# A two-layer hybrid trunk: the last 64 of 320 small triangular inverses go from VectorE to GpSimd

## The chip, the cores and the metric

The kernel runs on one core of a Trainium2 chip. A core has a matrix engine (TensorE, PE in the rows below), a vector engine (VectorE, DVE), an activation engine (ScalarE, ACT), a general-purpose vector engine (GpSimd, POOL), and SyncE (SP), which here issues the DMA transfers. Each engine works through its own list of instructions in order and waits on semaphores for the others. The metric is device time in microseconds (us), the median of several runs; lower is better.

## The reference, cut to what matters

Two layers are applied to 1024 latent tokens and 256 context tokens of width 1024. Each layer has a token mixer with three parallel head groups, an output projection, and a SwiGLU block. Of the mixer two groups matter here: the windowed attention, whose queries and keys are rotated, and a recurrence with a 64x64 state per head, in both directions.

```
def apply_rope(x, cos, sin):
    ...
    out = jnp.stack([x1 * c - x2 * s, x2 * c + x1 * s], axis=-2)
...
    def update(S, w_t, k_t, v_t, kk_t, a_t):
        sa = jnp.einsum('bhvk,bhk->bhv', S, kk_t)
        return (S * w_t[:, :, None, :] - sa[..., None] * (kk_t * a_t)[:, :, None, :]
                + v_t[..., None] * k_t[:, :, None, :])
...
    _, y_f = wkv_scan(wX[:, :, 0], kdX[:, :, 0], vX, kkX, aX[:, :, 0], Sc_f, False, rX)
    _, y_b = wkv_scan(wX[:, :, 1], kdX[:, :, 1], vX, kkX, aX[:, :, 1], Sc_b, True, rX)
```

The kernel doesn't step token by token. It takes 64 tokens at a time; inside such a chunk the updates are coupled by a unit lower triangular matrix, and its inverse turns the chunk into a few matmuls. The inverses are built from the inverses of 32x32 diagonal blocks, 320 of them per layer.

## The kernel before, in words

In each layer the mixer runs in this order: projections; attention over 16 to 20 units (one tile of 128 query tokens and one key head each); the recurrence over 80 units; the output projection. The recurrence has four chains (two head pairs by two directions), each of five groups of 256 tokens, each group of four chunks: unit 0 to 19 is chain 0, 60 to 79 chain 3. So one unit is one chunk for a pair of heads, and group 5 holds units 20 to 23, group 6 units 24 to 27, group 7 units 28 to 31.

A unit has four stages that are issued at different steps: u0 (the matmuls that start a unit, their masks on DVE at L1230 and L1233), u1, u4 and u5 (the state update, whose scaling on DVE is L1267). Tiles of a group are `bC`: three sets of them are used in turn. `beta_load` issues a group's loads on SP (L1201 and L1203 from `cb`, L1204 from `tb`, L1210 from `vt`), and it may be issued only when the inverses of its chain are joined; `own` then copies parts of them on POOL (L1182). `chunk_set` makes the constant parts of a set (DVE L1165, POOL L1167 and L1174).

Two lanes of background work are woven into attention and recurrence. The second lane makes the inverses: `elim(b0, n)` loads `n` blocks, one block per partition (`eL<-Ld`, L662), lays an identity into `eX` (POOL L663, L664), and runs 31 steps of forward elimination. Step j multiplies a column of the block by a row of the inverse so far (L671, of (31-j)(j+1) elements per partition) and subtracts the product (L673). Each of the 62 operations needs the result of the one before it. Then `eX` is stored (L675), its transpose copied to `eL` (L676), and that is stored (L677). `join_load` reads the results back (L696 to L699), and `join` puts pairs of 32x32 blocks together on PE (tile `gg` during the recurrence, 32x32 matmuls) and stores them to `tb` (L718). `inverses` calls elim for blocks 0 to 127, 128 to 255, and, ahead of join 6, for blocks 256 to 319. Joins 6 and 7, which read these, belong to chain 3 alone.

Attention of unit n takes its queries from `rot`: two multiplications on DVE (L959, L960) and one addition on POOL (L962, 128x256). PE transposes the rotated queries (L1053), then makes the scores, DVE their maximum (L1085), ACT the exponential, DVE part of the scaling (L1109); PE transposes the result (L1132) and multiplies by the values.

What the program text writes is not the order in which the engines work. A scheduler sets the order of each engine's list when the kernel is built, from its own idea of what an instruction costs and needs; on the chip each list is then run as it stands.

Of the kernel before, what the change touches and what calls it, by code (L numbers as in the profile page):

```python
# [13 lines left out]
ALU = mybir.AluOpType  # L14
# [80 lines left out]
def trunk(ctx: ExitStack, tc: tile.TileContext, x, ctxt, cc, w_mod, pp, w_in, w_out, lng, lnb, sgw, sink,  # L95
          w2, a2, g2, w_gu, w_down, cst, rope, out, dbg=None):
    nc = tc.nc
    V, S, G, T, D = nc.vector, nc.scalar, nc.gpsimd, nc.tensor, nc.sync
# [14 lines left out]
    def alloc(name, dt=F32):  # L113
        i = free.popleft()
        return Slot(sp.tile([128, NTOK], dt, tag=f"s{i}", name=nm(name)), i)

    def rel(*ss):
        for s in ss:
            free.append(s.i)
# [420 lines left out]
    def layer(l):  # L540
# [114 lines left out]
            rel(L1, L2, O1, O2)  # L655
            yield AC

        def elim(b0, n):

            ML = alloc("eL")  # L660
            MX = alloc("eX")
            D.dma_start(ML.t[:n, :1024], Ld[b0:b0 + n].rearrange("s i j -> s (i j)"))  # L662
            G.memset(MX.t[:n, :1024], 0.0)  # L663
            G.memset(MX.t[:n, 0:1024:33], 1.0)  # L664
            Lm = ML.t[:n, :1024].rearrange("p (i j) -> p i j", j=32)
            X = MX.t[:n, :1024].rearrange("p (i j) -> p i j", j=32)
            yield EW
            for j in range(31):
                r, c = 31 - j, j + 1
                tmp = ML.t[:n, 1024:1024 + r * c].rearrange("p (i j) -> p i j", j=c)  # L670
                V.tensor_tensor(tmp, Lm[:, j + 1:, j:j + 1].to_broadcast([n, r, c]),  # L671
                                X[:, j:j + 1, :c].to_broadcast([n, r, c]), op=ALU.mult)
                V.tensor_tensor(X[:, j + 1:, :c], X[:, j + 1:, :c], tmp, op=ALU.subtract)  # L673
                yield EC
            D.dma_start(Xd[0, b0:b0 + n, :], MX.t[:n, :1024])  # L675
            V.tensor_copy(Lm, X.rearrange("p i j -> p j i"))  # L676
            D.dma_start(Xd[1, b0:b0 + n, :], ML.t[:n, :1024])  # L677
            rel(ML, MX)
            yield
# [3 lines left out]
        def join_load(n):  # L683

            ci, c0 = n // 2, 10 * (n % 2)
            J = alloc("jT")

            def v(b, c, w=320):
                return J.t[h32[b], c:c + w].rearrange("p (c j) -> p c j", c=10)

            def xb(z, b):
                m = (ci * 20 + c0) * 4
                return Xd[z, m:m + 40].rearrange("(c b) (i j) -> b i c j", b=4, i=32)[b]
            for lo, hi in ((0, 1), (2, 3)):
                G.memset(v(lo, 0, 640)[:, :, 32:64], 0.0)
                D.dma_start(v(hi, 640), c10(Ad[ci][h32[hi], c0 * 32:c0 * 32 + 320]))  # L696
                D.dma_start(v(hi, 960), xb(1, hi))
                D.dma_start(v(lo, 0, 640)[:, :, 0:32], xb(0, lo))
                D.dma_start(v(hi, 0, 640)[:, :, 32:64], xb(0, hi))  # L699
            return n, J, v  # L700

        def join(n, J, v):
            for st_ in range(2):
                ps = x_t()
                for c in range(10):
                    for lo, hi in ((0, 1), (2, 3)):
                        o = slice(32 * c, 32 * c + 32)
                        if st_ == 0:
                            mm(ps[h32[lo], o], v(hi, 640)[:, c, :], v(hi, 960)[:, c, :])
                        else:  # L710
                            mm(ps[h32[hi], o], v(lo, 640)[:, c, :], v(lo, 0, 640)[:, c, 0:32])
                yield
                for lo, hi in ((0, 1), (2, 3)):
                    if st_ == 0:
                        S.activation(v(lo, 640), c10(ps[h32[lo], 0:320]), AF.Copy)
                    else:
                        S.activation(v(hi, 0, 640)[:, :, 0:32], c10(ps[h32[hi], 0:320]), AF.Copy, scale=-1.0)
            D.dma_start(tb[n // 2][:, (n % 2) * 640:(n % 2) * 640 + 640], J.t[:, 0:640])  # L718
            rel(J)
# [9 lines left out]
        def inverses():  # L729
            for pair in range(2):  # L730
                while ("alpha", pair) not in rw:
                    yield
                yield from elim(128 * pair, 128)
            j = join_load(0)
            for n in range(8):
                if n == HB:
                    while "beta" not in rw:
                        yield
                    j = join_load(n)
                if n == 6:  # L740
                    yield from elim(256, 64)
                    j = join_load(n)
                i, j = j, join_load(n + 1) if n not in (HB - 1, 5, 7) else None
                yield JW
                yield from join(*i)
                if n % 2:
                    rw["join", n // 2] = True
# [64 lines left out]
        def mix_done(i, raw, dst, begun=False):  # L812
            lat = i < 3 and not full
            token_mix(l, i, raw.t, dst.t, lat, begun)
            rel(raw)
            if i in (3, 4):
                bgq.appendleft(kk_norm(i - 3, dst))
            elif i in (0, 1):
                spill(dst, i, 2, 256 if lat else 0)
                rw["r", i] = True  # L820
            elif i == 7:
                S.activation(dst.t, dst.t, AF.Tanh)
                rw["wd"] = dst
            elif i == 8:
                rw["ad"] = dst
            elif i in (5, 6):
                D.dma_start(rd[i - 5], dst.t)
                bgq.appendleft(v_turn(i - 5, dst))
            else:
                c0 = 256 if lat else 0  # L830
                D.dma_start(rd[2][:, c0:], dst.t[:, c0:])
                rel(dst)
            if i == 0:
                bgq.append(alphas())
                elq.append(inverses())
# [547 lines left out]
        for n in range(len(ul) + max(s[1] for s in LG)):  # L1383
# [4 lines left out]
            for s, lag in LG:  # L1388
                m = n - lag
                if 0 <= m < len(ul):  # L1390
                    ci, gi, c = ul[m]
# [409 lines left out]
        tmp, aux = ft, alloc("aux")  # L1801
# [176 lines left out]
```

## Time and profile before

| what | value |
| --- | --- |
| time, median of 3 runs | 3263.41 us (3260.81 to 3267.21) |
| the profiled execution's own time | 3260.54 us |
| its span, first to last instruction | 3258.5 us |
| mean granted TensorE clock | 0.987 of full speed |
| busy share PE / DVE / ACT / POOL | 97% / 62% / 43% / 16% |
| elim of the last 64 blocks, layer 0 | 530.3 to about 587 us |
| elim of the last 64 blocks, layer 1 | 2259.4 to about 2308 us |
| last unit's query rotation on POOL, layer 0 | 541.20 us |
| first unit of the recurrence on PE, layer 0 / 1 | 566.35 / 2259.16 us |

Busy shares are averages over the whole span. In the rows below, times are us from the start of the span; a form such as 64x207 is 64 partitions by 207 elements, and a row's bracket gives how long the engine had been idle and what ended that.

### The profile page before, as it was taken

What the parts mean: (1) busy time and instruction counts of PE and PEld (TensorE: products, weight loads), DVE (VectorE), ACT (ScalarE), POOL (GpSimd) and SP (SyncE); (2) the same over time, 40 slices, a digit from 0 to 9 for tenths busy, and PEclk for the clock granted to TensorE, in tenths of its full rate; (3) what the DMA queues carried; (4) which work ended last, traced back from release to release, by engine and by line L of the source; (5) the groups of instructions that cost most, each with busy time, mean ns of one, the idle gap of its engine ahead of it and who ended that gap; (6) DMA issues with size and microseconds to landing.
All of it is one profiled execution on the core that took longest, in us unless ns stands there. A gap on an engine that the chain in (4) does not pass through costs nothing.

```text
span 3258.5 us, 51944 instructions
## 1 busy us (share of the span) xinstructions
PE 3152.4 (97%) x19892; PEld 2560.8 (79%) x19892; DVE 2004.0 (62%) x3966; ACT 1389.1 (43%) x2874; POOL 527.9 (16%) x598
## 2 busy tenths in 40 slices
PE   7999999999999999999999999999899999999998
PEld 4868887777788888886687788887677788888887
DVE  3448878775465555554455656886665666666556
ACT  4455577664332222222112556576564423333211
POOL 2300101232012222210001220111122122231000
PEclk9999999999999999999999999998999999999999
DMA  6477223346512122235722357313445222223332
GB/s 223 147 237 246 72 78 95 105 132 207 199 49 68 64 72 70 70 132 198 250 86 91 112 176 235 124 54 91 119 134 195 72 78 82 87 80 134 99 102 97
DMA packets 395175, 403.95 MB, mean 124 GB/s; under 512 B 113456, under 2 KB 334640, under 8 KB 394928
## 3 DMA queue, kind: packets, MB, share of 16 engines
q1 hardware_dynamic: 394928, 400.64, 38.3%
q8 instruction: 157, 2.57, 0.3%
q14 instruction: 90, 0.74, 0.1%
HBM read 279.97 MB, written 120.59 MB: 123 GB/s over the span
## 4 chain that ended last, share of the span: by engine, by line
PE 66%; DVE 6%; ACT 2%; DMA 1%; issue 1%; POOL 1%; SPq 0%; DVEq 0%; POOLq 0%; ACTq 0%
PE dd L148 25%; PE mm L148 19%; PE xx L148 15%; PE u L148 4%; PE mm L1132 1%; PE gg L148 0%; DVE yac L1711 0%; DVE eX L673 0%; POOL ss L180 0%; DVE eL L671 0%; DVE xr L1740 0%; DVE mx L483 0%; DMA ar<-actd 0%; PE xx L1132 0%; DVE yac L1739 0%
## 5 line engine op out<-in xcount | busy, mean ns | idle before, releaser
L148 PE MATMUL mm<-h,wh 128*128 128x512 f32 (+1 forms) x1424 | 421.7, 379 | 3.3 <-ACT ntmp L402 2.3
L148 PE MATMUL mm<-wh,h 128*128 128x256 f32 x1472 | 324.7, 295 | 1.3 <-ACT gel L872 0.6
L148 PE MATMUL dd<-h,wh 128*128 128x256 f32 (+1 forms) x1312 | 323.1, 337 | 2.7 <-DVE h L411 2.0
L148 PEld LDWEIGHTS mm<-h,wh 128*128 128x128 f32 x1424 | 258.5, 190 | 63.0 <-issue 13.7
L148 PE MATMUL mm<-h,wl 128*128 128x512 f32 (+1 forms) x712 | 266.3, 374 | 1.1 <-DVE wl L233 1.1
L148 PEld LDWEIGHTS mm<-wh,h 128*128 128x128 f32 x1472 | 247.8, 192 | 18.7 <-issue 14.7
L148 PEld LDWEIGHTS dd<-h,wh 128*128 128x128 f32 x1312 | 228.7, 191 | 31.2 <-DVE h L411 2.5
L1589 ACT ACTIVATE wh<-wq 128x1024 fp32r<-128x1024 f32 x114 | 121.0, 1062 | 302.8 <-PE dd L148 113.9
L148 PE MATMUL dd<-h,wl 128*128 128x256 f32 (+1 forms) x656 | 220.1, 336 | 0.0
L1590 DVE TENSOR_TENSOR wl<-wq,wh 128x1024 fp32r<-128x1024 f32 x114 | 141.2, 1238 | 114.8 <-ACT wh L1589 114.8
L148 PE MATMUL mm<-wl,h 128*128 128x256 f32 x736 | 210.3, 286 | 0.5 <-DVE wl L233 0.5
L148 PE MATMUL dd<-tt,wh 128*128 128x512 f32 x608 | 188.1, 391 | 0.0
L180 POOL TENSOR_TENSOR ss<-ss,mh_sb 128x1 f32<-128x1 f32 x74 | 50.4, 682 | 842.4 <-DVE ss L379 840.1
L148 PEld LDWEIGHTS mm<-h,wl 128*128 128x128 f32 x712 | 135.1, 190 | 25.2 <-DVE wl L233 1.4
L1711 DVE TENSOR_TENSOR yac<-yac,mm 128x512 f32<-128x512 f32 x126 | 86.4, 686 | 107.9 <-PE mm L148 107.5
L148 PEld LDWEIGHTS mm<-wl,h 128*128 128x128 f32 x736 | 142.0, 193 | 2.5 <-issue 1.4
L1711 DVE TENSOR_TENSOR yac<-yac,xx 128x512 f32<-128x512 f32 x126 | 86.3, 685 | 91.2 <-PE xx L148 91.1
L1579 POOL TENSOR_TENSOR wq<-wu 128x512 f32<-128x512 f32 x38 | 49.2, 1295 | 562.1 <-DVE wl L1590 478.1
L148 PEld LDWEIGHTS dd<-h,wl 128*128 128x128 f32 x656 | 125.3, 191 | 12.5
L148 PE MATMUL u<-bC,bC 128*128 128x128 f32 (+1 forms) x640 | 124.2, 313 | 9.5 <-DVE bC L1233 6.3
L148 PEld LDWEIGHTS dd<-tt,wh 128*128 128x128 f32 x608 | 111.7, 188 | 21.3
L148 PE MATMUL dd<-tt,wl 128*128 128x512 f32 x304 | 118.3, 389 | 0.0
(372 smaller groups left out, 7779.7 us busy)
## 6 DMA issues: line engine op xcount, KB each, us to landing
wm<-in_w_mod SPq DMA_DIRECT2D x80, 512.0 KB, 5.4
wr<-in_w_down SPq DMA_DIRECT2D x44, 512.0 KB, 4.4
wr<-in_w_in SPq DMA_DIRECT2D x38, 512.0 KB, 4.4
cb<-ao SPq DMA_DIRECT2D x76, 256.0 KB, 3.0
wu<-in_w_gu SPq DMA_DIRECT2D x38, 512.0 KB, 3.7
wq<-in_w_gu SPq DMA_DIRECT2D x38, 512.0 KB, 3.7
ao<-rk SPq DMA_DIRECT2D x58, 256.0 KB, 3.8
xs<-xr SPq DMA_DIRECT2D x28, 512.0 KB, 2.6
```

Source lines behind the costliest of these rows:

```text
L148: T.matmul(o, lhsT=lhsT, rhs=rhs, start=start, stop=stop, skip_group_check=parts)
L180: G.tensor_tensor(dst, src, mh[:, :n], op=ALU.pow)
L1132: T.transpose(ps[:, z * 128:(z + 1) * 128], P[i // 2].t[:, c:c + 128], ident)
L1579: G.tensor_tensor(a[:, 0:512], u[:, 0:512], u[:, 512:1024], op=ALU.add)
L1589: S.activation(w.hi[i], raw[i], AF.Copy)
L1590: V.tensor_tensor(w.lo[i], raw[i], f32(w.hi[i]), op=ALU.subtract)
L1711: V.tensor_tensor(yac[t].t[:, c], yac[t].t[:, c], ps, op=ALU.add)
```

## The change

`elim` gets the engine as an argument, and the call for the last 64 blocks passes GpSimd, in both layers. The two other calls are unchanged.

```
-        def elim(b0, n):
+        def elim(b0, n, E=V):
...
-                V.tensor_tensor(tmp, Lm[:, j + 1:, j:j + 1].to_broadcast([n, r, c]),
+                E.tensor_tensor(tmp, Lm[:, j + 1:, j:j + 1].to_broadcast([n, r, c]),
                                 X[:, j:j + 1, :c].to_broadcast([n, r, c]), op=ALU.mult)
-                V.tensor_tensor(X[:, j + 1:, :c], X[:, j + 1:, :c], tmp, op=ALU.subtract)
+                E.tensor_tensor(X[:, j + 1:, :c], X[:, j + 1:, :c], tmp, op=ALU.subtract)
...
-            V.tensor_copy(Lm, X.rearrange("p i j -> p j i"))
+            E.tensor_copy(Lm, X.rearrange("p i j -> p j i"))
...
                 if n == 6:
-                    yield from elim(256, 64)
+                    yield from elim(256, 64, G)
```

The scheduler sets new orders on every engine. Three places matter for what follows. The first is POOL's list in layer 0, at the end of attention, as the difference between the two lists. The list enters this piece with 36 of the 62 operations of elim already behind the memsets of `eX`; `q` is the query tile of the last attention unit.

```order
+L671 TENSOR_TENSOR eL_5868<-eL_5868,eX_5869 64x247
+L673 TENSOR_TENSOR eX_5869<-eX_5869,eL_5868 64x13x19
 L962 TENSOR_TENSOR q_3391<-q_3391 128x256
 L1182 COPY bC_6059<-bC_6062 64x2x4x64
 L1182 COPY bC_6060<-bC_6062 64x2x4x64
+L671 TENSOR_TENSOR eL_5868<-eL_5868,eX_5869 64x240
+L673 TENSOR_TENSOR eX_5869<-eX_5869,eL_5868 64x12x20
 L1182 COPY bC_6011<-bC_6014 64x2x4x64
```

So 38 operations of elim now stand ahead of the last unit's rotation, and 24 behind it, where there were none before.

The second is PE's list of the changed kernel at the same place: `xx_6044` takes the transposed queries of that last unit, `dd` are scores and `P` the probabilities of the unit before it.

```order
L148 MATMUL xx_5923<-PT_5959,Vt_2904 64x256 x4
L148 MATMUL xx_5923<-PT_5985,Vt_2904 64x256 x2
L1053 MATMUL xx_6044<-cst_sb,q_3391 128x128 x4
L148 MATMUL dd_6024<-kh_4595,qs_3392 128x384
L148 MATMUL dd_6024<-kh_4595,qs_3392 128x256
L148 MATMUL dd_6024<-kl_4596,qs_3392 128x384
L148 MATMUL dd_6024<-kl_4596,qs_3392 128x256
L1132 MATMUL mm_6052<-cst_sb,P_5876 128x128
```

The transposes stand where they stood before, ahead of the remaining scores of the unit before and of everything that follows.

The third is SP's list in layer 1, some 20 units into the recurrence, as a difference. `bC_21582` and `bC_21583` are tiles of group 5, `Xd` is where elim stores its results.

```order
+L1201 DMA bC_21582<-cb_16396 64x8x64
+L675 DMA Xd_16402<-eX_21657 64x1024
+L677 DMA Xd_16402<-eL_21656 64x1024
+L1201 DMA bC_21582<-cb_16396 64x8x64
+L1203 DMA bC_21583<-cb_16396 128x256
 L1204 DMA bC_3130_22012<-tb_16400 128x256
 L1210 DMA bC_3130_22012<-vt_16395 64x4x128
-L1201 DMA bC_21582<-cb_16396 64x8x64 x2
-L1203 DMA bC_21583<-cb_16396 128x256
```

Half of group 5's loads now stand behind the stores of elim's results. Further on, group 6's loads stood ahead of those stores and now stand behind the store of join 6 (L718), and group 7's moved behind the store of join 7. On PE, in the same stretch, the 80 small matmuls of joins 6 and 7 now all stand ahead of unit 24's first matmul:

```order
+L148 MATMUL gg_22091<-jT_22044 32x32 x19
+L148 MATMUL u_3197_22442<-bC_3130_22012,U_21591 64x64 x2
+L148 MATMUL gg_22114<-jT_22044 32x32 x20
+L148 MATMUL u_3201_22463<-bC_3130_22012,U_21591 64x64 x2
+L148 MATMUL gg_22190<-jT_22055 32x32 x20
+L148 MATMUL gg_22213<-jT_22055 32x32 x20
+L148 MATMUL u_3189_22401<-bC_21221,bC_21220 128x128 x2
```

The last row is the first of unit 24; before, the joins' matmuls lay between the stages of units 24 to 27.

## Rows read from the trace of the kernel before

**Rows 1.** The page, part 1: busy time, share of the span, instructions of each engine
```profile
PE 3152.4 (97%) x19892; PEld 2560.8 (79%) x19892; DVE 2004.0 (62%) x3966; ACT 1389.1 (43%) x2874; POOL 527.9 (16%) x598
```

**Rows 2.** Windows: length, busy PE PEld DVE ACT POOL, clock, DMA share, GB/s
```profile
2279.90:2309.10 29.20, 23.13 (x205) 17.67 (x206) 27.67 (x98) 14.05 (x52) 4.61 (x7) 0.97 0.50 137
588.00:601.00 13.00, 13.00 (x123) 9.75 (x121) 8.26 (x32) 7.72 (x31) 0.20 (x1) 1.00 0.31 54
```

**Rows 3.** Timeline of DVE, L1267, layer 0, units 0, 6, 12, 22: start, duration
```profile
573.29 0.28 DVE L1267 TENSOR_SCALAR bC<-u,pc 64x64 f32<-64x64 f32 x1
...
588.49 0.28 DVE L1267 TENSOR_SCALAR bC<-u,pc 64x64 f32<-64x64 f32 x1 [0.33 <-PE u L148]
...
600.96 0.28 DVE L1267 TENSOR_SCALAR bC<-u,pc 64x64 f32<-64x64 f32 x1
...
628.51 0.28 DVE L1267 TENSOR_SCALAR bC<-u,pc 64x64 f32<-64x64 f32 x1 [0.65 <-PE u L148]
```

**Rows 4.** Windows, DVE's work on eX alone: length, busy, clock, DMA share, GB/s
```profile
530.20:587.00 56.80, 21.79 (x63) 1.00 0.48 137
2259.30:2308.30 49.00, 21.64 (x63) 0.79 0.44 124
```

**Rows 5.** Timeline of POOL, layer 0, end of attention
```profile
529.86 0.38 POOL L664 MEMSET eX<- 64x32 f32 x1
531.32 0.24 POOL L1167 COPY bC<-cst_sb 128x64 f32<-128x64 f32 x1 [1.08 <-PE mm L148]
...
536.33 1.41 POOL L1174 COPY bC<-cst_sb 64x512 f32<-64x512 f32 x1 [2.87 <-PE mm L148]
...
541.20 0.73 POOL L962 TENSOR_TENSOR q<-q 128x256 f32<-128x256 f32 x1 [3.16 <-DVE q L960]
...
559.16 0.61 POOL L1174 COPY bC<-cst_sb 64x512 f32<-64x512 f32 x1 [5.05 <-ACT P L1098]
```

**Rows 6.** Timeline of POOL: two-input instructions, back to back
```profile
113.24 0.74 POOL L891 TENSOR_TENSOR v<-v,gw 128x256 f32<-128x256 f32 x1 [0.38 <-ACT v L890]
114.06 0.74 POOL L892 TENSOR_TENSOR v<-v,gw 128x256 f32<-128x256 f32 x1
...
969.73 1.29 POOL L1579 TENSOR_TENSOR wq<-wu 128x512 f32<-128x512 f32 x1 [42.35 <-DVE tt L1550]
971.10 1.30 POOL L1580 TENSOR_TENSOR wq<-wq,wq 128x512 f32<-128x512 f32 x1
```

**Rows 7.** POOL's groups by line: busy us, mean ns, idle before
```profile
L1182 POOL COPY bC<-bC 64x512 f32<-64x512 f32 x72 | 46.7, 649 | 129.8 <-PE u L148 70.3 <-DMA bC<-cb 56.2 <-issue 0.9
L1182 POOL COPY bC<-bC 64x256 f32<-64x256 f32 x8 | 3.4, 424 | 6.1 <-PE u L148 5.9
```

**Rows 8.** Timeline of PE, layer 0: last queries transposed, first unit
```profile
542.88 0.49 PE L1053 MATMUL xx<-cst_sb,q 128*128 128x128 f32 x3
...
566.35 1.16 PE L148 MATMUL u<-bC,bC 128*128 128x128 f32 x8
```

**Rows 9.** Timeline of DVE, layer 1: L1267, ten units apart
```profile
2279.89 0.28 DVE L1267 TENSOR_SCALAR bC<-u,pc 64x64 f32<-64x64 f32 x1 [1.39 <-PE u L148]
...
2309.08 0.28 DVE L1267 TENSOR_SCALAR bC<-u,pc 64x64 f32<-64x64 f32 x1
```

**Rows 10.** Timeline of SP's queue, layer 1
```profile
2307.09 0.49 SPq L675 DMA_DIRECT2D Xd<-eX  x1
...
2328.86 0.34 SPq L718 DMA_DIRECT2D tb<-jT  x1
```

**Rows 11.** Timeline of DVE, layer 1: first mask of units 24 and 28
```profile
2324.21 0.29 DVE L1230 TENSOR_TENSOR U<-u,cst_sb 128x128 f32<-128x128 f32 x1 [0.35 <-PE u L148]
...
2342.28 0.29 DVE L1230 TENSOR_TENSOR U<-u,cst_sb 128x128 f32<-128x128 f32 x1 [3.60 <-PE u L148]
```

**Rows 12.** Windows, layer 1, around unit 28: columns as in Rows 2
```profile
2335.00:2340.00 5.00, 2.42 (x66) 1.86 (x60) 1.12 (x4) 3.33 (x12) 0.00 (x0) 0.95 0.36 116
2340.00:2345.00 5.00, 3.98 (x18) 3.43 (x19) 1.78 (x7) 0.54 (x2) 2.44 (x4) 0.50 0.81 215
```

## The prediction, made before the changed kernel had run

> **What bounds the kernel now.** I read the page's busy shares first, then the windows around the two stretches in which the last 64 blocks are eliminated, then the timelines of the engines there. PE is busy 97% of the span and POOL 16% [rows 1], but that is an average: the change touches about 57 us in layer 0 and 49 us in layer 1 [rows 4], and what it is worth is read there. In layer 1 the elimination runs beside the first 20 units of the recurrence. DVE is busy 27.67 of 29.20 us, PE 23.13 [rows 2]: DVE is the bound, and ten units take 2309.08 - 2279.89 = 29.2 us, 2.92 each [rows 9]. Where no elimination is left, in layer 0 from unit 6 on, PE is busy 13.00 of 13 us [rows 2] and six units take 600.96 - 588.49 = 12.5 us, 2.08 each; the six before, with the end of the elimination in them, took 15.2 us, 2.53 each [rows 3]. In layer 0 most of the elimination lies ahead of the recurrence, beside the last attention units.
>
> **Part 1, what DVE is rid of.** 63 instructions, 21.8 us in layer 0 and 21.6 us in layer 1 [rows 4]. In layer 0 units 0 to 22 took 628.51 - 573.29 = 55.2 us [rows 3]; 22 units at the PE-bound pace would take 45.8, a gain of up to 9.4. The joins that stretched the later ones stay, so I take 7. In layer 1 the ten units at 2.92 would save 10 x 0.84 = 8.4 us at that pace, as far as the units may run ahead (part 4).
>
> **Part 2, what POOL is given.** No row shows these operations on POOL, so I bound them by the nearest. The operations of step j have (31-j)(j+1) elements: 62 of them with 10,912 elements together, of which the first 38 have 7,220. Two-input instructions follow each other on POOL by 0.82 us at 256 elements and 1.37 at 512 [rows 6], so one costs 0.28 + 0.00213 n us. That makes 62 x 0.28 + 10,912 x 0.00213 = 40.6 us per layer, against DVE's 21.7, and 26.0 us for the first 38. The lower bound is the one-input copy, 424 ns at 256 and 649 at 512 [rows 7], 0.20 + 0.00088 n, about 12.7 us for the first 38 and some 20 for all. These operations have inner rows of 1 to 31 elements, half of them broadcast, where the nearest rows have long ones; for that, and for DVE beside it, I take one and a half times the middle as the upper bound, 61 us and 39. I take 40.6: the operation has two inputs, as the rows of 6 have.
>
> **Part 3, who waits in layer 0.** 38 of the 62 now stand ahead of the last unit's rotation. POOL is free for them at 529.86 + 0.38 = 530.24 [rows 5]. With 26.0 us of them, two copies of 0.24 and one of 0.61 between [rows 5] and 0.73 for the rotation itself, it ends at 558.1, where it ended at 541.9. Beside DVE a copy of this kind took 1.41 us instead of 0.61 [rows 5]; I add one such delay, 0.8, and some slack, and take 560. Queued behind the rotation are two copies of `own`; behind its reader, the transposes on PE, stands everything that is left of attention: remaining scores of the unit before, probabilities, values. PE is in order and can do none of it. The transposes began at 542.88 [rows 8], so they come 17.1 us late. From them to the recurrence's first matmul there were 23.5 us [rows 8]; DVE is rid of 8 us of elimination in these, and a part of what the softmax waits for, I take 21. So the first unit starts at 581 instead of 566.35, 14.6 us late. The idle PE costs clock: in layer 1, after 5 us with PE busy 2.42, the granted clock was 0.50 for 5 us in which PE was busy 3.98 [rows 12], which cost about 2 us of work; after 17 idle us I take 3. Layer 0: 14.6 + 3 - 7 = +10.6.
>
> The Trainium skill's page "SBUF — State Buffer", section "Who interferes with whom", holds that a DVE instruction with two SBUF inputs contends with a GpSimd instruction that reads SBUF, and that in a two-port mode whoever issues first holds the ports for the whole instruction. The 1.41 us copy ran beside a DVE subtraction with two SBUF inputs, so the row agrees. By the page alone each of DVE's scalings and subtractions in this stretch could be added to POOL's chain, an estimate of some 4 us in place of the 0.8; the sum would then be +13 instead of +10. I go by the row.
>
> **Part 4, who waits in layer 1.** The elimination starts at about 2259.4 there, behind the load of its blocks. With 40.6 us of it and four 0.65 us copies of `own` between [rows 7] it ends at 2302.6, and the first store leaves at 2302.8, where it left at 2307.09 [rows 10]. So the results are ready 4 us sooner, though POOL needs twice as long as DVE, because the interleaving no longer spreads them. But the units are quicker too: at 2.08 from unit 8 on, unit 20 wants its loads at about 2310, and half of group 5's now wait behind the two stores. The transposing copy (1.1 us at the rate of [rows 7]) ends at 2304, and with the same 5 us the loads land at about 2309: just in time. Group 6's loads wait for join 6's store, which needs loads of `jT` and two rounds of 32x32 matmuls with ACT copies between. Before, that store left 2328.86 - 2307.09 = 21.8 us after the first store of elim [rows 10]; from 2302.8 that gives 2324.6, and with some 5 us, which I take for the loads behind it, unit 24's first mask comes at about 2330, where it was at 2324.21; unit 28, which stalled 3.60 us for loads behind join 7's store, at 2342.28 [rows 11], comes at about 2341. What DVE's relief wins ahead of unit 20 is waited for at unit 24, and the stall at unit 28 shrinks: I take -1 for layer 1.
>
> **Sum.** +10.6 - 1 = +9.6 us on the profiled execution's 3260.54, 3270. The median of the runs is 2.9 us above the profiled execution, so I predict 3273 us.
>
> **Rivals.**
>
> POOL is as quick on these as on copies. Then the 38 operations take 12.7 us, the rotation ends at 530.2 + 12.7 + 1.1 + 0.7 = 544.7, 3 us late, and the shorter chain behind it makes up for that; layer 0 wins the 7 us, and layer 1, whose results are ready at about 2282, before any load waits for them, some 4. That is -11, 3252 us, faster. It decides from a mean of about 0.42 us per operation ahead of the rotation (548 less 1.8 less 530.2, over 38): up to 548 the delay is no longer than the 7 us won. For it speaks that one-input rows are this short [rows 7], against it that all two-input rows of POOL are slower [rows 6]. The Trainium skill's page "GPSIMD Engine Reference", section "Elementwise — side-by-side cycle accounting", puts a two-input operation at about 2.6 cycles per element, a floor set by its read port; rows 6 agree with that in slope, 2.13 ns per element, and so it speaks against this rival, an estimate of 23.6 us for the elements alone.
>
> POOL is slower than its long rows suggest, by half: 39 us ahead of the rotation, which ends at 572, 30 us late; the first unit comes 27 us late, with the clock +30, less 7 is +23. In layer 1 the elimination ends at 2323, joins 6 and 7 hold unit 24 until about 2350, and some 6 of these 25 us come back at unit 28: +19. Together +42, 3304 us. For it speak the short broadcast rows, for which the trace has no example; against it, that DVE takes the same short rows without a penalty that shows.
>
> The recurrence gives everything back. The late start stands, but the chain behind the transposes shrinks to 19 (DVE and POOL no longer share the elimination there), all units run at 2.08 (-9.4), and layer 1 wins 4: 17.1 - 4.5 + 3 - 9.4 - 4 = +2, about 3264. For it speaks that PE is the bound as soon as the elimination is gone [rows 2]; against it, that the joins still have to be fitted in.
>
> **How the numbers follow.** The forecast has 0.55, with its own range 3262 to 3284; the quick POOL 0.12, the slow POOL 0.13, the recurrence that gives all back 0.20. A measurement of this kernel can tell about 0.2%, 6.5 us, from no change. Faster comes from the quick POOL and the edge of the last rival, 0.14; no change from most of the last rival and the lower third of the forecast, 0.32; slower 0.54. The range 3252 to 3298 reaches down to the quick POOL and most of the way to the slow one.
>
> **What would show it.** The rotation L962 of layer 0's last unit near 559, not 541; PE idle ahead of L1053 by some 13 to 17 us, and a row of granted clock 0.5 behind it; the first unit near 581 to 584; units at about 2.1 us from the start. On POOL, L671 and L673 following each other by 0.28 + 0.00213 n, 0.82 at 256 elements. In layer 1 `Xd<-eX` issued near 2303, unit 24's first mask near 2330, relative to a first unit at 2259. The forecast is wrong if POOL's spacing is under 0.45 or over 0.95 on average ahead of the rotation, if the scheduler's order let PE work on other tiles while it waits for the rotation, or if unit 24 is not held by the joins.

## The result, and the profile after

The changed kernel takes 3279.12 us (median of 6 runs, 3272.47 to 3292.63) against 3263.09 us before (3255.66 to 3267.21): ratio 1.0055, 95% interval 1.0039 to 1.0070: slower by 16 us in the medians, by some 18 in the ratio. The forecast was slower, 3273 us, +9.6 on the profiled execution.

The profiled execution of the changed kernel is the longest of its six, 3292.6 us, span 3290.5. Of the 32 us between the two spans 9.0 lie ahead of everything the change touches (the rotation ahead of the elimination starts at 536.86 instead of 527.84) and 7.0 between the recurrences, so I compare the lengths of stages, not absolute times. Busy shares say little, as before; the page's part 1:

```profile
PE 3166.1 (96%) x19892; PEld 2574.4 (78%) x19892; DVE 1969.4 (60%) x3840; ACT 1386.9 (42%) x2874; POOL 590.7 (18%) x724
```

The timeline of POOL at the end of layer 0's attention answers to [rows 5] and, for the spacing, to [rows 6]:

```profile
539.34 0.25 POOL L671 TENSOR_TENSOR eL<-eL,eX 64x31 f32<-64x31 f32 x1
...
545.69 1.40 POOL L673 TENSOR_TENSOR eX<-eX,eL 64x175 f32<-64x175 f32 x1
...
559.51 0.64 POOL L671 TENSOR_TENSOR eL<-eL,eX 64x256 f32<-64x256 f32 x1
560.22 0.72 POOL L673 TENSOR_TENSOR eX<-eX,eL 64x256 f32<-64x256 f32 x1
561.02 0.63 POOL L671 TENSOR_TENSOR eL<-eL,eX 64x255 f32<-64x255 f32 x1
...
565.24 0.71 POOL L962 TENSOR_TENSOR q<-q 128x256 f32<-128x256 f32 x1
```

The rotation ends 26.6 us after the elimination has begun; at 256 elements two operations take 1.51 us. Then the timeline of PE, the answer to [rows 8]:

```profile
566.01 1.12 PE L1053 MATMUL xx<-cst_sb,q 128*128 128x128 f32 x4 [13.27 <-POOL q L962]
...
595.23 3.68 PE L148 MATMUL xx<-PT,Vt 128*64 128x256 f32 x16 [7.13 <-ACT PT L1137]
598.84 1.18 PE L148 MATMUL u<-bC,bC 128*128 128x128 f32 x8
```

These are two waits, and only the first was forecast. The second is followed back through the timelines of ACT, POOL and SP:

```profile
594.09 0.60 ACT L1313 ACTIVATE gsx<-gsx,hw 128x256 f32<-128x256 f32 x1 [7.42 <-POOL gsx L1308]
594.60 1.06 ACT L1137 ACTIVATE PT<-mm 128x512 f32<-128x512 f32 x2
```

```profile
593.34 0.72 POOL L1308 TENSOR_TENSOR gsx<-gsx 128x256 f32<-128x256 f32 x1 [7.30 <-DMA gsx<-td]
```

```profile
582.34 0.48 SPq L675 DMA_DIRECT2D Xd<-eX  x1
584.37 0.48 SPq L677 DMA_DIRECT2D Xd<-eL  x1
584.94 0.54 SPq L1152 DMA_DIRECT2D od<-attO  x1
...
589.42 0.60 SPq L1294 DMA_DIRECT2D gsx<-td  x1
```

SP stood until 582.34 at the store of elim's result; in its waits that is this row (what waits, for what, us in total, times, longest):

```profile
SPq L675 <- POOL eX L673: 13.9, 1, 13.9
```

Behind that store stand loads and stores of the attention and of the recurrence, among them the load of `gsx`, a tile of the recurrence's output work (`rw_out`). ACT's list has an activation of `gsx` ahead of the last two copies of the attention's probabilities. In the kernel before, it stood about 150 instructions behind them, and came 73 us after they had begun (562.94):

```profile
635.93 0.60 ACT L1313 ACTIVATE gsx<-gsx,hw 128x256 f32<-128x256 f32 x1
```

So the last attention unit waits for a tile that has nothing to do with it.

DVE's scaling L1267, the answer to [rows 3], for units 0, 6 and 23. The last unit of a chain has no state update and so no such row: there are 76 rows for 80 units, and the row that [rows 3] puts down to unit 22 is that of unit 23.

```profile
604.08 0.28 DVE L1267 TENSOR_SCALAR bC<-u,pc 64x64 f32<-64x64 f32 x1
...
615.33 0.28 DVE L1267 TENSOR_SCALAR bC<-u,pc 64x64 f32<-64x64 f32 x1
...
653.31 0.28 DVE L1267 TENSOR_SCALAR bC<-u,pc 64x64 f32<-64x64 f32 x1
```

Unit 0 comes 21.8 us late (604.08 - 573.29 - 9.0). Units 0 to 23 take 49.2 us instead of 55.2, and from the first to the last such row of the layer it is 179.3 instead of 186.6: 7.3 us come back.

In layer 1 the timeline of DVE, the scaling of units 0 and 14 and the first mask of unit 24 (the answer to [rows 11]), then SP's store ([rows 10]), then the window behind unit 14 (columns as in [rows 2]):

```profile
2299.14 0.28 DVE L1267 TENSOR_SCALAR bC<-u,pc 64x64 f32<-64x64 f32 x1 [0.73 <-PE u L148]
...
2330.37 0.28 DVE L1267 TENSOR_SCALAR bC<-u,pc 64x64 f32<-64x64 f32 x1
...
2366.11 0.29 DVE L1230 TENSOR_TENSOR U<-u,cst_sb 128x128 f32<-128x128 f32 x1 [7.85 <-PE u L148]
```

```profile
2329.89 0.48 SPq L675 DMA_DIRECT2D Xd<-eX  x1
```

```profile
2330.00:2370.00 40.00, 33.16 (x329) 27.06 (x328) 11.59 (x43) 14.12 (x50) 5.57 (x8) 0.54 0.42 102
```

14 units take 31.2 us instead of 42.2, and the store leaves 30.8 us behind unit 0 instead of 38.5. Then it is all taken back, with the joins ahead of unit 24 and the granted clock at 0.54 over 40 us; unit 24's mask comes 67.0 us behind unit 0, before 55.6: first to last row 198.3 us, 194.7 before.

### The profile page after: what moved, and what is told of

It reads as the page before. It is cut to its first block, busy times and chain, and to the rows that moved or that the text cites. A ratio compares the mean times of both kernels' runs of the same rounds, so it can differ in the third digit from the quotient of the medians.

```text
span 3290.5 us, 51965 instructions
## 1 busy us (share of the span) xinstructions
PE 3166.1 (96%) x19892; PEld 2574.4 (78%) x19892; DVE 1969.4 (60%) x3840; ACT 1386.9 (42%) x2874; POOL 590.7 (18%) x724
## 4 chain that ended last, share of the span: by engine, by line
PE 70%; DVE 5%; DMA 2%; ACT 2%; issue 1%; POOL 1%; SPq 1%; DVEq 0%; POOLq 0%; ACTq 0%
PE dd L148 25%; PE mm L148 19%; PE xx L148 15%; PE u L148 8%; PE gg L148 1%; PE uy L148 1%; PE mm L1132 1%; DVE yac L1711 0%; POOL ss L180 0%; DVE xr L1740 0%; DVE mx L483 0%; DMA ar<-actd 0%; PE xx L1132 0%; DVE yac L1739 0%; DMA wm<-in_w_mod 0%
## 5 line engine op out<-in xcount | busy, mean ns | idle before, releaser
L148 PEld LDWEIGHTS mm<-h,wh 128*128 128x128 f32 x1424 | 261.4, 192 | 64.3 <-issue 14.5
L148 PEld LDWEIGHTS mm<-wh,h 128*128 128x128 f32 x1472 | 249.0, 193 | 18.9 <-issue 14.1
L148 PEld LDWEIGHTS dd<-h,wh 128*128 128x128 f32 x1312 | 228.1, 191 | 30.8 <-DVE h L411 2.3
L1085 DVE CUSTOM_DVE_ANT_0 P<-dd,cst_sb 128x640 f32<-128x640 f32 (+2 forms) x128 | 95.1, 753 | 44.5 <-PE dd L148 33.9
```

The costliest lines, as they stand in the source:

```text
L148: T.matmul(o, lhsT=lhsT, rhs=rhs, start=start, stop=stop, skip_group_check=parts)
L1085: V.tensor_tensor_reduce(out=po, in0=pi, in1=m, scale=1.0, scalar=-3.0e38, op0=ALU.add, op1=ALU.max, accum_out=mx[:, h:h + 1])
```

## The experiments

Each ratio is against the kernel before, with its 95% interval; the timelines are of each run's own profile. In runs that add lines, line numbers are up to 6 higher than in the listing.

**One layer at a time.**

```
-                    yield from elim(256, 64, G)
+                    yield from elim(256, 64, V if l else G)     # layer 0 only
+                    yield from elim(256, 64, G if l else V)     # layer 1 only
```

> Only layer 0's last 64 blocks go to GpSimd. The changed kernel is 1.0055, layer 1 alone 0.999: if the two add up, layer 0 alone is 1.005 to 1.007, with the first unit some 21 us late and 7 us of it won back by unit 79. If the two layers do not add up (the later one catches up with nothing), 1.004 or less.

> Only layer 1's last 64 blocks go to GpSimd; layer 0 keeps them on VectorE. In the trace of the changed kernel layer 0 loses some 14.5 us from the start of attention's end to the last unit (first unit 21.8 us late, 7.3 us of it won back by unit 79), layer 1 loses 3.6 us. If layer 0 is where the time goes (first and second theory alike), this kernel is within 4 us of the one before, ratio 1.000 to 1.001. If the long half-clock stretch of layer 1 (40 us behind unit 15) is the real price, the ratio stays near the changed kernel's 1.0055.

Layer 0 alone: 1.0060 (1.0041 to 1.0079). Layer 1 alone: 0.9990 (0.9978 to 1.0002), 193.3 us for its recurrence against 194.7. The cost is layer 0's: it is there whole without layer 1's change, and layer 1 alone is even with the kernel before or a little ahead.

Single profiles can't tell differences of a few us between recurrences. In the run of layer 1 alone, every engine's list in layer 0 is the same as before, and yet its recurrence took 193.7 us instead of 186.6. One place where it was slower, as windows (columns as in [rows 2]), the kernel before first:

```profile
700.00:710.00 10.00, 10.00 (x84) 7.14 (x80) 7.17 (x23) 6.22 (x21) 2.18 (x4) 1.00 0.29 81
```

```profile
700.00:710.00 10.00, 10.00 (x62) 7.55 (x62) 6.24 (x20) 4.22 (x14) 4.12 (x5) 0.66 0.19 52
```

**The last rotation on VectorE.**

```
-                rot(ps[:, 0:256], q[:, 0:256], 4, t - 2, q[:, 256:512])
+                rot(ps[:, 0:256], q[:, 0:256], 4, t - 2, q[:, 256:512], V if n == N - 1 else G)
```

> As changed, but the last attention unit's rotary addition runs on VectorE in both layers, so it stands behind no operation of elim. First theory (the forecast's): the 13.3 us in which PE waits for that addition are the cost in layer 0; the ratio falls from 1.0055 to about 1.0015. Second theory: attention's end hangs on the end of elim all the same, because ACT's last copies of the attention stand behind an activation of gsx whose loads stand on SP behind elim's two stores; the PE wait moves there (7.1 us becomes about 20), the first unit starts as late as before, and the ratio stays at 1.005.

1.0055 (1.0039 to 1.0072): nothing gained. PE's timeline, then ACT's:

```profile
545.34 0.60 PE L1053 MATMUL xx<-cst_sb,q 128*128 128x128 f32 x4
...
586.11 3.68 PE L148 MATMUL xx<-PT,Vt 128*64 128x256 f32 x16 [19.92 <-ACT PT L1137]
```

```profile
584.98 0.60 ACT L1313 ACTIVATE gsx<-gsx,hw 128x256 f32<-128x256 f32 x1 [20.21 <-POOL gsx L1308]
```

The transposes no longer wait, and nearly all of the 13.3 us turns up at the other wait: 7.1 became 19.9. The forecast's mechanism is real and yet, taken away alone, is worth nothing.

**The stores on GpSimd's own queue.**

```
-            D.dma_start(Xd[0, b0:b0 + n, :], MX.t[:n, :1024])
+            (G if E is G else D).dma_start(Xd[0, b0:b0 + n, :], MX.t[:n, :1024])
```

and the same for the second store.

> As changed, but the two stores of the 64 blocks are issued by GpSimd instead of SyncE, so nothing waits behind them on SP. Both theories: PE still waits 13 us for the rotation in layer 0. If the 7.1 us wait of ACT for gsx comes from SP's queue, the gsx addition on GpSimd now runs right behind elim (about 2 us after it instead of 11), and the wait falls by 6 to 7 us: ratio about 1.0035. If it comes from GpSimd's own order alone, nothing changes: 1.0055. In layer 1 group 5's loads no longer stand behind the stores: up to 2 us more.

1.0042 (1.0025 to 1.0059), between the two expected values. PE's second wait falls from 7.1 to 4.6 us, not to 0 or 1. SP now waits at another place:

```profile
SPq L1294 <- DMA Xd<-eL: 7.9, 1, 7.9
```

```profile
584.88 3.68 PE L148 MATMUL xx<-PT,Vt 128*64 128x256 f32 x16 [4.62 <-ACT PT L1137]
```

The load of `gsx` itself waits for the store of `eL`: `gsx` is given the buffer that `eL` had, out of a pool that all these tiles share.

**Rotation, stores and gsx all moved.** Also the first `gsx` addition and multiplication on VectorE.

```
-            G.tensor_tensor(s1, s1, s2[:, ::-1], op=ALU.add)
+            (V if c0 == 0 else G).tensor_tensor(s1, s1, s2[:, ::-1], op=ALU.add)
```

> As changed, with the stores on GpSimd's queue, the last rotary addition on VectorE and the first gsx addition and multiplication of the recurrence's output on VectorE: nothing of attention's end waits for elim any more. First and second theory together: layer 0's first unit starts no later than before, the recurrence keeps the 7 us it won, layer 1 as changed (+2 to +4): ratio 0.998 to 1.000. If GpSimd's work slows VectorE beside it (third theory, contention), attention's end is still late by several us: 1.002 or more.

1.0032 (1.0021 to 1.0043), a miss. The buffer of `eL` is still shared, and the next run, which changes that alone, gains the rest; no timeline of this run is used.

**Elim's tiles kept, so that gsx has its own buffer.** On top of the last one, on the changed kernel alone, and with the last rotation on VectorE:

```
-            rel(ML, MX)
+            if E is V:
+                rel(ML, MX)
+            else:
+                held.extend((ML, MX))     # released behind the last join
```

> As the run with all three freed, and the two tiles of elim are kept until the joins are done, so that gsx gets another slot and its loads no longer wait for elim's last store. Theory now: two waits of layer 0 stood beside each other, PE for the last rotation and ACT for gsx, both behind the end of elim, and removing one leaves the other. With both gone the first unit starts within 3 us of before, the recurrence keeps its 7 us, layer 1 wins 0 to 3: ratio 0.996 to 0.999. Rival (GpSimd's work slows VectorE or GpSimd's other work by contention, whatever the order): the first unit is still 8 us or more late, ratio 1.002 or more.

> As changed, but elim's two tiles are kept until the joins are done, so gsx has another slot. The rotation stays behind 38 operations of elim. Theory of the two waits: the 13.3 us wait of PE for the rotation stays, the 7.1 us wait of ACT for gsx goes; the first unit is some 14 us late instead of 21.8: 7 us less than the changed kernel, ratio about 1.003. Rival (the rotation is not a cost by itself since it is caught up later): first unit under 5 us late, ratio 1.000.

> As changed, with the last rotation on VectorE and elim's tiles kept; the stores stay on SyncE's queue and the gsx addition on GpSimd. Theory of the two waits: both are gone, first unit within 3 us of before, ratio 0.997 to 1.000, where the last rotation alone brought nothing (1.0055) and the slot alone some 7 us. If loads that stand on SP behind elim's stores matter by themselves, the first units stall for them and the ratio is 1.002 to 1.004.

The slot alone: 1.0020 (1.0010 to 1.0030). As expected, PE's wait for the rotation stays and the one for `gsx` is gone; no other wait of PE at attention's end is longer than 2.3 us:

```profile
556.09 1.11 PE L1059 MATMUL xx<-cst_sb,q 128*128 128x128 f32 x4 [13.15 <-POOL q L968]
...
579.74 1.16 PE L148 MATMUL u<-bC,bC 128*128 128x128 f32 x8
```

From the transposes to the first unit it is 23.7 us; the unit starts 14.0 us late (579.74 - 566.35, and 0.6 for an earlier start), and 5.9 come back by the last one.

Slot and rotation: 1.0042 (1.0030 to 1.0054), worse than the slot alone, against the expectation of 0.997 to 1.000. Attention ends in time, and the recurrence then stalls at its third unit. DVE, then SP:

```profile
589.77 0.29 DVE L1236 TENSOR_TENSOR U<-u,cst_sb 128x128 f32<-128x128 f32 x1 [16.98 <-DMA od<-attO]
```

```profile
576.09 0.48 SPq L677 DMA_DIRECT2D Xd<-eX  x1
...
588.26 0.38 SPq L1158 DMA_DIRECT2D od<-attO  x1
```

A third tile waits: `U` takes the buffer of an attention output whose store stands on SP behind elim's stores. With everything freed it is 1.0000 (0.9987 to 1.0014), where 0.996 to 0.999 was expected. The first unit's matmul on PE is on time (570.84 - 566.35, less 4.3 for the later start of the units ahead of it, is 0.2 us). Elim runs on POOL beside it all the while, so the rival, that POOL's work slows attention's end by contention, is out:

```profile
570.84 1.16 PE L148 MATMUL u<-bC,bC 128*128 128x128 f32 x8
```

A piece of the third wait is still there, since a load of a later unit, which takes elim's buffer in its turn, stands on SP ahead of the same attention store (DVE, then SP's waits):

```profile
585.99 0.29 DVE L1236 TENSOR_TENSOR U<-u,cst_sb 128x128 f32<-128x128 f32 x1 [12.59 <-DMA od<-attO]
```

```profile
SPq L1210 <- DMA Xd<-eX: 19.3, 1, 19.3
```

So layer 0 is not free of cost even there: in this profile its last scaling comes 7.9 us late (the same 4.3 taken off), and layer 1's recurrence is 5.0 us shorter than before.

**Elim begun when attention is over.**

```
                 if n == 6:
+                    while "beta" not in rw:
+                        yield
                     yield from elim(256, 64, G)
```

> Both layers on GpSimd, but elim of the last 64 blocks starts when attention is over. No attention work can wait for it; in layer 0 it lies beside the first 20 units, as in layer 1. Theory (the cost is that attention's end waits for elim on GpSimd): layer 0's first unit starts no later than before, units run at about 1.9 us, of which some is given back at the joins: ratio 0.996 to 0.999. Rival (elim on GpSimd costs wherever it stands, through loads behind its stores): 1.001 or more.

1.0058 (1.0041 to 1.0075): the theory that attention's end is what pays was too narrow. The first unit's matmul is on time, but layer 0's recurrence takes 212.1 us instead of 186.6. ACT, then PE:

```profile
606.20 0.60 ACT L1315 ACTIVATE gsx<-gsx,hw 128x256 f32<-128x256 f32 x1 [16.73 <-POOL gsx L1310]
```

```profile
607.45 1.22 PE L148 MATMUL u<-bC 128*128 128x128 f32 x4 [15.95 <-ACT bC L1245]
```

Now the addition of `gsx` stands on POOL behind elim's operations, ACT stands at the activation behind it, and the recurrence behind ACT. Of the 25.5 us 16 are this wait; most of the others are lost ahead of unit 28, with the granted clock at 0.51 from 640 to 650. Layer 1 computes no output for the context tokens, has no `gsx` among its first units, and takes 193.1 us in the same run.

**16 of the 31 steps, layer 0 only.** The other 15 are left out.

```
-            for j in range(31):
+            for j in range(31 if E is V else 16):
```

> Layer 0 only, and GpSimd runs 16 of the 31 steps of elim; the other 15 are left out. Same engine, same tiles, same waits, but elim is over some 20 us sooner. Theory (everything that waits in layer 0 waits for elim's end, which comes later than the order of the engines allows for): first unit within 4 us of before, ratio 0.997 to 1.000. Rival (the moved order itself costs, whatever elim takes): first unit 10 us or more late, ratio 1.003 or more.

1.0029 (1.0015 to 1.0044), half the cost, where I expected none. POOL, then PE:

```profile
556.04 1.89 POOL L676 COPY eL<-eX 64x1024 f32<-64x1024 f32 x1
557.90 0.71 POOL L962 TENSOR_TENSOR q<-q 128x256 f32<-128x256 f32 x1
```

```profile
558.67 1.12 PE L1053 MATMUL xx<-cst_sb,q 128*128 128x128 f32 x4 [10.89 <-POOL q L962]
```

The scheduler put all 32 operations, and the copy as well, ahead of the rotation, so that wait fell only to 10.9 us; the ACT wait, behind elim's end, is gone. The first unit is 12.3 us late. By the signs set beforehand that speaks for the rival, the moved order; but as elim's end and the order moved together, the run neither separates the theories nor contradicts the two waits.

**Layer 1 alone, joins later, and their stores on ScalarE.** Layer 1 only, stores on GpSimd's queue, and ahead of join 6:

```
+                    if l:
+                        yield 30
...
-            D.dma_start(tb[n // 2][:, (n % 2) * 640:(n % 2) * 640 + 640], J.t[:, 0:640])
+            (S if l and n > 5 else D).dma_start(tb[n // 2][:, (n % 2) * 640:(n % 2) * 640 + 640], J.t[:, 0:640])
```

The first run has only the later joins, the second the stores as well.

> Layer 1 only, stores on GpSimd's queue, and joins 6 and 7 put some ten units later in the program, so that they lie between units 24 and 32 instead of all ahead of unit 24. If the joins in front of unit 24 give back what VectorE's relief wins (10.6 us by unit 14, of which 7.4 are lost by unit 27), a good half of that is kept: ratio 0.996 to 0.998. If it is the half clock behind unit 15 that gives it back, it stays at the 0.999 of layer 1 alone.

> As the run of layer 1 with late joins, and the stores of joins 6 and 7 are issued by ScalarE, right behind the copies they wait for, so that no load stands behind them on SP. There the recurrence was 14 us ahead at unit 27 and had lost it by unit 75, with SP standing 8.5 us at those stores. If that wait gave it back, most of 14 us is kept: ratio 0.996 to 0.998, faster than before and than the changed kernel. If something else in units 27 to 75 did (the output work that follows sooner), it stays at 1.000.

Later joins alone: 1.0007 (0.9993 to 1.0021), nothing gained; units 0 to 28 take 65.4 us instead of 79.6, but the whole recurrence 201.2 instead of 194.7. With the stores on ScalarE: 3256.18 us, 0.9981 (0.9969 to 0.9993), some 6 us faster than before, and faster than the changed kernel. DVE's scaling of units 0, 14 and 28, and a store on ScalarE's queue:

```profile
2271.63 0.28 DVE L1269 TENSOR_SCALAR bC<-u,pc 64x64 f32<-64x64 f32 x1 [0.73 <-PE u L148]
...
2302.60 0.28 DVE L1269 TENSOR_SCALAR bC<-u,pc 64x64 f32<-64x64 f32 x1
...
2332.03 0.28 DVE L1269 TENSOR_SCALAR bC<-u,pc 64x64 f32<-64x64 f32 x1
```

```profile
2330.14 0.35 ACTq L718 DMA_DIRECT2D tb<-jT  x1
```

It is 60.4 us to unit 28 and 188.8 in all: the ratio is in the expected range, but of the 19 us won by unit 28 (the expectation's unit 27, counted by rows) only 5.9 are kept. 8.4 of the other 13 are lost between units 29 and 42, in which the clock was low:

```profile
2340.00:2350.00 10.00, 10.00 (x46) 7.73 (x45) 4.04 (x13) 2.09 (x7) 0.71 (x2) 0.54 0.71 217
```

The kernel before has such a stretch ahead of unit 29 ([rows 12]: 0.50 from 2340 to 2345), so a part of the lead at that point is only that the low clock comes later. What takes the rest stays open.

## Why the prediction was right, and the step that was not

- **The direction and the mechanism of part 3 held.** The rotation stands behind 38 operations of elim and PE waits 13.3 us for it. The 38 take 24.6 us (565.24 - 539.34, less 1.3 for the four small instructions between) where I had 26.0. The transposes come 14.1 us late (566.01 - 9.0 - 542.88), 17.1 in the forecast, of which some 2 were slack and a delay. But the direction did not rest on this wait alone: without it the kernel is as slow (1.0055), as the other wait takes its place. The forecast did not have that.
- **The step that failed** is the chain behind the transposes, which I put at 21 us instead of 23.5. It was 32.8 (598.84 - 566.01), 9.4 more than before: 7.1 us of it the wait of ACT for `gsx`, and 1.7 the lower clock behind that wait (the 16 matmuls at 595.23 took 3.68 us, before 1.95). So the first unit's matmul comes 23.5 us late where I had 14.6, and at 589.8 (598.84 - 9.0) instead of the 581 to 584 that I had named as a sign. I had followed SP's queue in layer 1 and not in layer 0, though its list moved there in the same way, and never ACT's. With that wait removed the chain is 23.7 us: DVE's relief, which I expected to shorten it, does not. The 16 matmuls before:

```profile
564.47 1.95 PE L148 MATMUL xx<-PT,Vt 128*64 128x256 f32 x16 [0.47 <-DVE PT L1139]
```

- **The recurrence of layer 0** was to give back 7: it gave 7.3 between the first and the last scaling, and 1.7 more ahead of the first. Layer 0's sum is then 14.1 + 9.4 - 1.7 - 7.3 = +14.5, forecast +10.6; layer 0 alone measures 1.0060, about 20 us. That the total came out within 6 us of the forecast is in part luck: the transposes were put 3 us too late, the chain behind them 9 too short, with the 3 for the clock counted to it.
- **Layer 1** was to be -1; alone it is 0.9990, -3 with an interval from -7 to +1. The course was as described: units at 2.2 us, elim's store earlier against unit 0 by 7.7 us where I had 4.3 (it ran 39.3 us with the copies between, not 43.2), then unit 24 held by the joins: 11.4 us later in the changed kernel where I had 6, but 6.9 in the run that begins elim later (62.5 us behind unit 0), whose lists in layer 1 are the same on every engine.
- **The clock** was not 3 us in one place. In layer 0 it was 0.50 behind each of the two waits (windows):

```profile
566.00:570.00 4.00, 3.99 (x19) 3.99 (x19) 1.52 (x3) 1.19 (x2) 3.74 (x7) 0.50 0.23 70
595.00:598.00 3.00, 2.77 (x14) 1.64 (x16) 0.00 (x0) 0.66 (x2) 0.49 (x1) 0.50 0.13 50
```

  In layer 1 two runs with the same work show its share. From unit 14 to unit 25, in the changed kernel and in the run that begins elim later:

```profile
2330.40:2375.10 44.70, 37.86 (x365) 30.76 (x366) 13.87 (x50) 16.62 (x60) 7.07 (x11) 0.58 0.46 116
```

```profile
2323.00:2362.30 39.30, 30.63 (x368) 24.89 (x367) 13.70 (x51) 16.28 (x60) 8.89 (x16) 0.74 0.52 132
```

  The same lists take 44.7 us at a clock of 0.58 and 39.3 at 0.74, and the whole recurrence 198.3 and 193.1. So the 3.6 us that layer 1 loses in the changed kernel's profile are not the price of its order; they go with the lower clock of that execution. Why the clock differs stays open.
- **The rivals.** Quick POOL is excluded: 0.65 us per operation on the first 38, where 0.42 was its bound. So is slow POOL, whose bound was 39 us for these 38. The recurrence did not give everything back.
- **Contention** was small, about 1.3 us on the first 38 operations: 0.9 on one subtraction, which took 1.40 us beside DVE's L233 where one of its size took 0.52 later, and 0.4 on two others. I had 0.8 from the row, and an estimate of 4 by the Trainium skill's page "SBUF — State Buffer", section "Who interferes with whom". That a DVE instruction with two SBUF inputs, as L233, contends with a POOL instruction that reads SBUF agrees with these rows:

```profile
545.14 1.56 DVE L233 TENSOR_TENSOR wl<-wr,wh 128x1024 fp32r<-128x1024 f32 x1
```

- **Slips in the working.** From the first scaling to that of [rows 3]'s fourth row are 23 units, not 22: at 2.08 they take 47.8 us, so the gain was bounded by 7.4, not 9.4. The rate of [rows 7] gives 14.0 and 22.0 us for the 38 and the 62 operations, not 12.7 and some 20. The two totals 3304 and 3264 come to 3305 and 3266. No row shows the 5 us taken for loads in part 4. None of these turns the forecast.

What the runs show together: in layer 0 several things wait side by side for elim on POOL, most of them for its end: the rotation (POOL's own list), all that stands on SP behind the stores, and the tiles that take over elim's buffers. Removing one moves the wait to the next (the rotation alone: 1.0055; the stores alone: 1.0042; rotation and buffer: 1.0042), and with all but one gone the kernel is even with the one before (1.0000), with a gain in layer 1 counted in. That the scheduler holds elim on POOL for shorter than it is on the chip would explain why it moved these rows forward; no run shows what it assumes.

## What to carry to other kernels

Work that is given to an idle engine is paid for by what stands behind it in order: on that engine, on the queue that issues its stores, and on every tile that takes its buffers next. Follow all three in every stage the change touches before you cost the move at nothing. When one wait is removed and the time does not move, look for a second wait for the same event before you call the first one harmless.

## What the runs showed of the hardware

On POOL these operations, with inner rows of 1 to 31 elements and broadcast inputs, cost no more than long rows: 0.71 to 0.80 us from start to start at 256 elements, against 0.82 in [rows 6], and 0.32 at 31. A transposing copy of 64x1024 on POOL took 1.9 us, not the 1.1 worked out from [rows 7]. In one place DVE and POOL, reading SBUF side by side, both took longer: 1.56 us instead of the 1.21 to 1.23 that L233 takes in most of its rows, and 1.40 instead of 0.52. The same lists took up to 7 us more or less in a recurrence from one execution to another, with the granted clock: 193.1 and 198.3 us in layer 1, 186.6 and 193.7 in layer 0.
